# One attention for two sequences, weight sums made on the spot, and a multiply that writes in order: a decoder layer on eight cores

## The chip, the cores and the metric

The kernel runs on all 8 cores of one Trainium2 chip; each core has two sequences of the batch of 16, with no traffic between cores. The time is that of the slowest core, in microseconds (us). An execution is called *slow* when the cores of one die show a lower granted TensorE clock and take over 1% longer than the other die's, or when it is over 1.5% above the fastest of its kernel; all others are *fast*. Only fast executions are compared, except where the text says otherwise.

In lines of the profile PE is TensorE (PEld its weight loads), DVE VectorE, ACT ScalarE, POOL GpSimd, SP the engine that issues most DMA loads and stores; "ps" are PSUM buffers, in which the matmuls leave their results, "M" other buffers. L1555 is line 1555 of the kernel. "A <- B: 32.0, 3, 16.4" says that A waited for B for 32.0 us in all, three times, the longest 16.4 us. The granted clock is the share of full speed at which TensorE was let run.

## The reference, cut to what matters

```python
D_MODEL, BATCH, SEQ, D_FF = 1024, 16, 2048, 2816

def swiglu(x, w_gate, w_up, w_down):
    return (jax.nn.silu(x @ w_gate) * (x @ w_up)) @ w_down

def reference(x, ...):
    h = swiglu(rms_norm(x, ffn1_pre_g), ffn1_w_gate, ffn1_w_up, ffn1_w_down)
    x = x + 0.5 * rms_norm(h, ffn1_post_g)
    # 4 differential heads (dense, causal) and 8 dilated heads; one projection in, one out
    h = hybrid_mixer(rms_norm(x, mix_pre_g), w_in, ..., w_out)
    x = x + rms_norm(h, mix_post_g)
    h = swiglu(rms_norm(x, ffn2_pre_g), ffn2_w_gate, ffn2_w_up, ffn2_w_down)
    return x + 0.5 * rms_norm(h, ffn2_post_g)
```

## The kernel before

Each feed-forward is done in two halves of 1024 tokens. A half is a *gate/up* stage and a *down* stage. Both multiply 2x2 blocks with seven products in place of eight (the Strassen-Winograd scheme), for which sums of weight blocks are needed. Those sums are either made on VectorE from weights just loaded ("raw"), or loaded from main memory, where an earlier stage has stored them. The attention has eight units: 0 to 3 are differential heads, 4 to 7 are pairs of dilated heads. A scheduler in the program places the instructions of each engine in a fixed order ahead of time.

The order of the stages, and the preparation of stored sums, which runs beside the attention:

```python
for s in range(NSEQ):
    half_ffn(s, 0, 0)
    half_ffn(s, 0, 1)
    push_prep(s)            # loads weights, makes sums on VectorE, stores them
    attention(s)
    need(("prep", s))
    half_ffn(s, 1, 0)
    half_ffn(s, 1, 1)
# ...
def push_prep(s):
    if s == 0:
        jobs = [(fi, "d", d, hf) for fi in (1, 0) for d in range(ND) for hf in range(2)]
        jobs += [(0, "g", l, 0) for l in UNSTORED]
    else:
        jobs = [(1, "g", l, 0) for l in UNSTORED]
```

The end of a dilated unit: sums of the exponentials and weighted values lie in PSUM in the order (r, i), with token = 4i + r. The reciprocal is exp(-ln(sum)); the multiply writes the mixed output in token order:

```python
for m in range(2):
    S.op(ACT, lambda e: e.activation(rec[lo], bank(4 + m)[hi], AF.Ln))
S.op(ACT, lambda e: e.activation(rec, rec, AF.Exp, scale=-1.0))
for m in range(2):
    S.op(DVE, lambda e: e.tensor_tensor(
        mixT[lo, u, ts(Q)].rearrange("p (i r) -> p r i", r=4),    # steps of 8 bytes
        bank(4 + m)[lo].rearrange("p (r i) -> p r i", r=4),
        rec[lo].rearrange("p (r i) -> p r i", r=4), ALU.mult))
```

The softmax here doesn't subtract the row's maximum and nothing guards it: scores larger than these inputs give would overflow.

## Time and profile before

| | |
|---|---|
| time, 4 runs | 3062.71 us median (3022.6 to 3089.92) |
| TensorE, VectorE, ScalarE, GpSimd busy | 86, 56, 47, 13% |
| two attentions, with the gap behind each, mean of the eight cores | 603.2 + 564.8 us |
| eight gate/up stages, sum of the cores' medians | 1173.5 us |
| eight down stages, sum of the cores' medians | 614.4 us |

A stage is taken from its first matmul to the first of the next stage, so that the idle time behind it belongs to it. The prediction shows the lines of the profile that these come from. The row of the normalising multiply (line, engine, operation, shapes, count | busy us, mean ns | idle before, and its causes), here of core 5:

```profile
L1555 DVE TENSOR_TENSOR M<-ps,M 64x512 f16<-64x512 f32 x64 | 82.9, 1295 | 108.0 <-ACT M L1551 88.3 <-PE ps L1204 10.8 <-ACT sml L1422 5.2
```

512 elements take 1295 ns, about 2.5 ns each: nearly twice the 688 ns that other operations of this size take (the casts of lines 1213 and 1254).

### The profile page before, as it was taken

How to read it: one execution, taken by the hardware profiler on the slowest of the kernel's cores; microseconds unless marked ns; L12 is line 12 of the kernel's file. 1: busy time of each engine (PE TensorE's matmuls, PEld its weight loads, DVE VectorE, ACT ScalarE, POOL GpSimd, SP SyncE). 2: the span in 40 equal slices, each digit the busy share in tenths (PEclk: the TensorE clock that was granted, in tenths of full speed). 3: DMA queues.
4: the chain of work that ended last, by engine and by line, in shares of the span. 5: the costliest groups of instructions: out<-in, count | busy, mean ns of one | idle time of the engine just before them, and what ended most of it. 6: DMA issues, size and time to landing. Idle time of an engine off the chain costs nothing.

```text
span 3059.0 us, 51439 instructions; the slowest of 8 cores (2993.8 to 3059.0 us)
## 1 busy us (share of the span) xinstructions
PE 2629.8 (86%) x16574; PEld 1345.0 (44%) x16608; DVE 1714.8 (56%) x2918; ACT 1435.0 (47%) x2186; POOL 398.8 (13%) x442
## 2 busy tenths in 40 slices
PE   5999898588986869988999999777898876999996
PEld 2444344355543423333444444654555542344455
DVE  5546634656664675458556465455445556534733
ACT  3434344486643733343354444446764465334432
POOL 1212210112010012102202112001110000110210
PEclk9999999799998977899999999998999998889998
DMA  7766954457477468566477675875212215636868
GB/s 160 153 145 142 187 97 95 108 129 149 90 151 177 108 156 182 162 158 152 122 228 226 199 239 174 269 183 141 75 26 41 44 49 177 188 115 198 268 181 263
DMA packets 241109, 466.94 MB, mean 153 GB/s; under 512 B 39632, under 2 KB 62416, under 8 KB 240848
## 3 DMA queue, kind: packets, MB, share of 16 engines
q1 hardware_dynamic: 203632, 362.90, 38.5%
q0 software_dynamic: 37216, 100.74, 21.1%
q8 instruction: 141, 2.31, 0.3%
q14 instruction: 120, 0.98, 0.1%
HBM read 447.10 MB, written 110.89 MB: 182 GB/s over the span
## 4 chain that ended last, share of the span: by engine, by line
PE 71%; DVE 10%; ACT 7%; issue 7%; DMA 4%; SPq 0%; DVEq 0%; another core or an unknown queue 0%; ACTq 0%; POOL 0%; POOLq 0%
PE ps L989 34%; PE ps L1056 12%; PE ps L1244 6%; PE ps L1092 5%; PE ps L1381 4%; PE ps L1204 3%; PE ps L1342 2%; ACT M L1364 2%; DMA sgu<-M 2%; PE ps L1279 2%; PE ps L1539 2%; ACT M L717 2%; DVE M L1555 2%; DVE M L789 1%; PE ps L1500 1%
## 5 line engine op out<-in xcount | busy, mean ns | idle before, releaser
L989 PE MATMUL ps<-M 128*128 128x512 f16 x4928 | 1150.0, 397 | 119.3 <-DVE M L866 48.9
L989 PEld LDWEIGHTS ps<-M 128*128 128x128 f16 x4928 | 495.5, 101 | 738.3 <-issue 301.2
L1056 PE MATMUL ps<-M 128*128 128x512 f16 (+1 forms) x2464 | 420.7, 333 | 38.5 <-DMA M<-sdn 18.7
L1364 ACT ACTIVATE M<-ps,btab 128x256 bf16<-128x256 f32 (+3 forms) x512 | 349.9, 712 | 141.9 <-PE ps L1342 116.9
L915 POOL TENSOR_TENSOR M<-M 128x512 f16<-128x512 f32 x176 | 234.4, 1332 | 1174.5 <-ACT M L911 1173.5
L719 DVE TENSOR_TENSOR M<-M 128x512 bf16<-128x512 bf16 x336 | 142.7, 425 | 378.4 <-ACT M L717 365.2
L1056 PEld LDWEIGHTS ps<-M 128*128 128x128 f16 x2464 | 244.8, 100 | 204.6 <-issue 56.4
L928 ACT ACTIVATE M<-ps 128x1024 f32<-128x1024 f32 x176 | 180.0, 1023 | 292.3 <-PE ps L989 286.3
L924 DVE TENSOR_TENSOR M<-M,ps 128x512 f16<-128x512 f32 x176 | 120.9, 687 | 317.4 <-PE ps L989 285.2
L1244 PE MATMUL ps<-M 128*128 128x512 f16 x1024 | 260.5, 391 | 32.5 <-DVE M L1444 10.6
L911 ACT ACTIVATE M<-M 128x512 f32<-128x512 f32 x176 | 110.6, 629 | 370.4 <-DVE M L932 370.4
L932 DVE TENSOR_TENSOR M<-ps,M 128x1024 f32<-128x1024 f32 x176 | 214.9, 1223 | 98.0 <-PE ps L989 97.8
L866 DVE TENSOR_TENSOR M<-M 128x1024 f16<-128x1024 f16 (+1 forms) x280 | 217.0, 793 | 61.6 <-DMA sgu<-M 36.3
L717 ACT ACTIVATE M<-M 128x512 bf16<-128x512 f32 (+1 forms) x280 | 165.0, 622 | 146.5 <-DVE M L808 85.8
L1507 ACT ACTIVATE M<-ps 128x1024 bf16<-128x1024 f32 x144 | 140.8, 1006 | 181.0 <-PE ps L1500 159.2
L1204 PE MATMUL ps<-M 128*128 128x128 f16 x2048 | 149.0, 226 | 44.4 <-DVE M L754 38.7
L1381 PE MATMUL ps<-M 128*128 128x129 bf16 x2176 | 177.0, 224 | 9.1 <-DVE M L1368 4.0
L1279 PE MATMUL ps<-M 128*128 128x512 f16 x512 | 126.1, 397 | 55.9 <-ACT M L713 26.0
L789 DVE SCALAR_TENSOR_TENSOR M<-M,gains 128x512 f16<-128x512 f16 x192 | 148.5, 793 | 22.0 <-ACT M L732 21.8
L1381 PEld LDWEIGHTS ps<-M 128*128 128x128 bf16 x2176 | 131.2, 99 | 66.2 <-issue 58.8
L754 DVE SCALAR_TENSOR_TENSOR M<-M,gains 128x512 f16<-128x512 f32 x192 | 132.1, 747 | 44.9 <-ACT M L732 44.6
L1092 PE MATMUL ps<-M 128*128 128x512 f16 x704 | 152.9, 379 | 0.2
(71 smaller groups left out, 2304.1 us busy)
## 6 DMA issues: line engine op xcount, KB each, us to landing
M<-sdn SPq DMA_DIRECT2D x224, 352.0 KB, 4.7
M<-sgu SPq DMA_DIRECT2D x308, 256.0 KB, 3.4
M<-wgu POOLq DMA_DIRECT2D x108, 512.0 KB, 8.0
M<-x SPq DMA_DIRECT2D x96, 512.0 KB, 8.1
sgu<-M SPq DMA_DIRECT2D x66, 512.0 KB, 6.8
M<-xT SPq DMA_DIRECT2D x64, 512.0 KB, 8.9
x<-M SPq DMA_DIRECT2D x64, 512.0 KB, 4.9
sdn<-M SPq DMA_DIRECT2D x48, 352.0 KB, 5.1
```

The lines of the kernel that those rows point to most:

```text
L717: S.op(ACT, lambda e: e.activation(sq[si], src, AF.Square), reads=rd, writes=[B_sq[si]], cost=c_act(512))
L866: eng, lambda e: e.tensor_tensor(SB(j), a, b, op), reads=rd, writes=[bS[j]], cost=cost),
L915: S.op(POOL, lambda e: e.tensor_tensor(hs(p, l), t[:, 0:512], t[:, 512:1024], ALU.mult), reads=bt, writes=[B_H[p][l]], cost=1.3)
L932: S.op(DVE, lambda e: e.tensor_tensor(o, bank(b, 2), o, ALU.add), reads=[B_ps[b], B_ps[b + 1]] + bo, writes=bo, cost=c_dve(1024))
L989: S.op(PE, lambda e, g=g, kc=kc, pb=pb, src=src, piece=piece, n=n: e.matmul(bank(pb + g), src[:, g * 512 + kc * 128:g * 512 + (kc + 1) * 1 ...
L1056: S.op(PE, lambda e, k=k, pb=pb, w=w, piece=piece, n=n: e.matmul(bk(pb), w.ap[:, k * 128:(k + 1) * 128], H[piece][:, k * 512 + c0:k * 512 ...
L1092: S.op(PE, lambda e, k=k, pb=pb, w=w, p=p, c=c: e.matmul(bank(pb), w.ap[:, k * 128:(k + 1) * 128], H[p][:, c * 512:(c + 1) * 512], start=( ...
L1204: S.op(PE, lambda e, kc=kc: e.matmul(bank(pb)[:, tq * 128:(tq + 1) * 128], xn[:, kc, t * 128:(t + 1) * 128], wap[:, kc * 128:(kc + 1) * 12 ...
L1244: S.op(PE, lambda e, kc=kc: e.matmul(bank(pb), wap[:, kc * 128:(kc + 1) * 128], xn[:, kc, ts(tt)], start=(kc == 0), stop=(kc == NKC - 1)), ...
L1279: S.op(PE, lambda e, k=k: e.matmul(bank(pb), wap[:, k * 128:(k + 1) * 128], mixT[:, k, ts(tt)], start=(k == 0), stop=(k == NKC - 1)), read ...
L1364: S.op(ACT, lambda e, o_=o_, i_=i_, bias=bias: e.activation(o_, i_, AF.Exp, bias=bias, scale=SCALE), reads=rd + [B_const], writes=[bP], co ...
L1381: S.op(PE, lambda e, a_ap=a_ap, m=m, uq=uq, first=first: e.matmul(a_ap, P[:, m, uq * 128:(uq + 1) * 128], Vt[i][:, kt, 0:w1], start=(kt == ...
```

## The change

Its intent: keep TensorE fed through the attention. All first feed-forwards come first, then one attention over both sequences, the second's projections filling the first's end, then all second feed-forwards. The preparation leaves the attention: the halves that work on raw weights store their sums. The plain (eight-product) down stages become seven-product ones. Cut to its core (scheduler, buffers and weight ring are left out):

```diff
-for s in range(NSEQ):
-    half_ffn(s, 0, 0); half_ffn(s, 0, 1)
-    push_prep(s); attention(s); need(("prep", s))
-    half_ffn(s, 1, 0); half_ffn(s, 1, 1)
+HALVES = [(s, fi, h) for fi in range(2) for s in range(NSEQ) for h in range(2)]
+RAW  = (tuple(range(NL)), (1, 3, 5, 7, 9), (3, 7), ())     # rows of blocks loaded raw, by half
+KEEP = ((0, 2, 4, 6, 8, 10), (1, 5, 9), (3, 7), ())        # of these, sums stored for later
+for i in range(len(HALVES)):
+    if i == 4: attention()                                  # both sequences
+    half_ffn(i)
+def raw_down(s, h, l):  return (s, h) == (0, 0) or ((s, h) == (0, 1) and l in (0, 2))
+def keep_down(s, h, l): return l in ((1, 3) if h == 0 else (0, 2))

+UORD = (4, 5, 0, 1, 2, 3, 6, 7)             # order of the units; was 0 to 7
+nxt_ = [(s + 1, u, tt) for tt in (lo, hi) for u in UORD[0:2]] if s + 1 < NSEQ else []
+blocks += [..., (s, 6, hi, nxt_[0:1]), (s, 7, hi, nxt_[1:])]

-S.dma_group(SP, prs, ...)                   # 256 copies of 24 KB, dilated values
+S.dma_group(POOL, prs, ...)

-e.activation(ya, bank(pb), AF.Copy)         # mixed output; later a f32 scalar-tensor-tensor
+e.activation(ya, bank(pb), AF.Copy, scale=gains[:, 24 + d:25 + d])   # later a f16 multiply

-    mixT[lo, u, ts(Q)].rearrange("p (i r) -> p r i", r=4),
-    bank(4 + m)[lo].rearrange("p (r i) -> p r i", r=4),
-    rec[lo].rearrange("p (r i) -> p r i", r=4), ALU.mult)
+    mixT[lo, u, ts(Q)].rearrange("p (i r) -> p i r", r=4),
+    bank(4 + m)[lo].rearrange("p (r i) -> p i r", r=4),
+    rec[lo].rearrange("p (r i) -> p i r", r=4), ALU.mult)
```

The four output buffers that the first attention used for its last tiles are taken out too, which leaves two.

## The prediction

> **What bounds the kernel now.** I read the core table first. It sets the yardstick: the time is that of the slowest core, and cores 2 and 3 are some 50 us behind the rest, at a lower granted clock. So I budget on core 5, which ran undisturbed (2993.8 us), and return to the clock at the end.
>
> ```profile
> core 2: 3059.0 us, clock 0.932
> core 3: 3055.1 us, clock 0.931
> core 5: 2993.8 us, clock 0.955
> ```
>
> Then the page's chain of work that ended last: TensorE carries 71% of it, and only in the feed-forward lines (989, 1056, 1092) does it run unbroken.
>
> ```profile
> PE 2629.8 (86%) x16574; PEld 1345.0 (44%) x16608; DVE 1714.8 (56%) x2918; ACT 1435.0 (47%) x2186; POOL 398.8 (13%) x442
> q1 hardware_dynamic: 203632, 362.90, 38.5%
> q0 software_dynamic: 37216, 100.74, 21.1%
> ...
> PE 71%; DVE 10%; ACT 7%; issue 7%; DMA 4%; SPq 0%; DVEq 0%; another core or an unknown queue 0%; ACTq 0%; POOL 0%; POOLq 0%
> ```
>
> The two queue rows (packets, MB, share of 16 engines) say what a byte costs: 0.385 x 3059 x 16 / 362.9 = 52 engine-us per MB on the hardware queue, and 102 on the software queue, whose loads halve f32 to f16. So such a load costs by its source bytes, and 16 engines move 16/52 = 308 MB per ms.
>
> Then core 5 cut at the stage borders (where TensorE's line changes). Columns: stretch, its length, busy time of each engine, clock, DMA share, GB/s.
>
> ```profile
> 32.10:180.50 148.40, 138.14 (x617) 60.16 (x618) 85.44 (x98) 58.66 (x78) 38.98 (x40) 0.99 0.75 161
> 180.50:257.00 76.50, 76.50 (x356) 34.69 (x355) 27.42 (x51) 28.83 (x51) 4.49 (x9) 1.00 0.49 93
> 481.80:1062.50 580.70, 455.77 (x4219) 265.85 (x4218) 349.46 (x702) 332.30 (x512) 65.03 (x94) 0.92 0.55 127
> 1062.50:1083.00 20.50, 1.58 (x19) 0.96 (x16) 11.81 (x22) 6.91 (x12) 0.53 (x1) 0.61 0.71 162
> 1552.40:1687.60 135.20, 133.72 (x620) 60.47 (x619) 82.40 (x117) 62.54 (x85) 29.37 (x22) 1.00 0.72 211
> 1687.60:1755.60 68.00, 66.99 (x311) 30.27 (x310) 34.10 (x63) 31.16 (x54) 0.12 (x1) 1.00 0.68 214
> 1890.70:1986.60 95.90, 73.68 (x621) 61.13 (x620) 48.97 (x97) 42.35 (x89) 3.34 (x7) 0.95 0.95 303
> ...
> 1986.60:2115.00 128.40, 93.18 (x859) 54.05 (x860) 68.79 (x164) 79.16 (x170) 14.27 (x22) 0.91 0.55 125
> 2115.00:2465.00 350.00, 305.01 (x3110) 185.89 (x3108) 190.55 (x373) 207.21 (x259) 24.84 (x35) 0.96 0.22 47
> 2465.00:2529.40 64.40, 50.73 (x250) 22.59 (x251) 39.48 (x70) 37.81 (x71) 0.00 (x0) 0.95 0.29 94
> ```
>
> A gate/up half with stored weight sums takes 135.2 us, 219 ns for each of its 616 matmuls: TensorE-bound. With weights loaded raw and summed on the spot it takes 148.4; a stored down pass 68.0, the plain one 76.5, one split into two column passes 95.9 with the DMA engines at 0.95. The attentions are bound by no engine: TensorE 449 of 543 us and ACT 324 in the second. The middle of it is 87% busy (305.0/350), its entry 73%, its exit 79%. After each come 20 us with TensorE almost empty.
>
> Last, what TensorE waits for from the first attention to the gap behind it:
>
> ```profile
> PE ps L725 <- DVE M L719: 32.0, 3, 16.4
> PE ps L1279 <- ACT M L713: 17.9, 1, 17.9
> PE ps L1539 <- DVE M L1555: 16.4, 17, 1.6
> PE ps L1204 <- DVE M L754: 9.6, 14, 2.5
> ```
>
> The first and last are norm chains at entry and exit; the second is the out-projection held while its buffer serves the weight preparation; the third a slow normalising multiply.
>
> [...]core 2: 0.82 from 2584 to 2773 us[...] cores 0 and 1 of that die had 1.00 and 0.99 then, and long dense stretches elsewhere run at 1.00. [...] 512 f16 elements take 420 ns, 512 f32 ones with a PSUM operand 687. [...]
>
> **The change part by part**, on core 5.
>
> *Order.* Both sequences' first feed-forward now come first, then one attention over both, then the second feed-forwards. The prenorm of the first sequence's attention input runs beside the last down pass; the second sequence's projections fill the first one's end; the second feed-forward's input is ready before attention ends. Today: 580.7 + 20.5 + 542.8 + 19.7 = 1163.7 us. If all attention work ran at the middle's rate: 2 x 448.9/0.871 = 1030. The normalising multiply now writes contiguously: 64 x 1294 ns today, against 687 for a like-sized one with contiguous output; I credit half its two waits of 16 us, 1030 - 16 = 1014. Add 15 us for one cold entry, the handover (the second sequence may not overwrite the mixed output before the first is projected) and the last out-projection: about 1030. Gain 134.
>
> *Preparation leaves attention.* It frees DVE there of about 36 us of 704-element and 34 us of 1024-element sums (64 x 567 ns; 40 x 860 ns); already inside the sum above, as the middle row has none.
>
> *Down passes.* Today: 76.5 + 76.3 (plain), 76.2, 69.2, 68.0, 95.9, 68.1, 78.7 = 608.9 (the third includes a wait at its end). After: eight seven-product passes, two-pass in the last only. The stored ones take 68, but the first half of each feed-forward takes four raw blocks and the second half two of four. Their four opening sums (1408 elements, about 1.1 us each by the 860 ns for 1024) stand on DVE before the second product: +2 to 3 us. Their DMA is heavy: by the program's shapes 11.5 MB of source weights, 5.0 MB stored and 4.2 MB of activations in about 70 us, which is 296 GB/s against the 308 above; I add 3 us more. So 73 + 72 + 68 + 68 and 74 + 72 + 68 + 78.7 = 573.7. Gain 35.
>
> *Gate/up.* Today 148.4 + 148.5 + 163.8 + 160.2 + 135.2 + 135.1 + 145.1 + 135.1 = 1171.4. A raw row of blocks costs (148.4 - 135.2)/11 = 1.2 us. After, the four halves have 11, 5, 2 and 0 raw rows: 149 + 141.5 + 137.5 + 135.2, and with 4 us more behind attention, where norm work remains: 153 + 141.5 + 137.5 + 135.2. Sum 1130.4. Gain 41.
>
> *Moved.* 256 small copies (24 KB) go from SP to GpSimd. At the 544 ns that GpSimd's issue of a projection load takes they are 140 us of an engine that is busy 104 of the two attentions' 1123 us: 9 us per group of 16, mostly while dilated units are projected ahead.
>
> *Sum.* Head and tail unchanged, 32.1 + 17.7 = 49.8; 49.8 + 1030 + 573.7 + 1130.4 = 2784. Other undisturbed cores lie up to 20 us above core 5: 2800. Today's throttled cores pay about 45 us for two returns from attention to dense matmuls (gate/up 184 and 170 instead of 164 and 145 on core 2); after there is one[...]. I add 10. **Predicted 2810 us**, 8% less.
>
> **The rivals.**
> *Attention does not merge well.* A static order, two buffers of Y instead of four, and the rule on overwriting could leave a new 20 to 40 us stall at the handover, or keep the mean at today's 83% (449/543), with 1080 to 1100 us in place of 1030. For it: the waits are many and short (17 on line 1555 in the first attention). Against: the long ones, 15 to 18 us each, are just those the new order removes. Time then 2860 to 2890.
> *DMA becomes the bound in the raw halves.* For it: 296 GB/s estimated against 308. Against: the ring holds two blocks' weights, so a load has about 17 us of lead. If each raw down pass rose to 85 us: +50, 2860.
> [...] each 160 us at 0.81 costs about 30 us. Then 2840 to 2870. [...]
> *GpSimd's copies delay diff units.* The square of line 1414 shares that queue with unit 6's copies; two groups of 9 us per sequence, at most 40 us, if DVE waits behind them.
>
> **Range and chances.** The gains sum to 210 us on one core; 2% needs 61. For less than that two rivals at full size would be needed together. One rival at full size gives 2890; everything going well (1000 for attention, no throttle) gives 2745. So 2745 to 2890, faster 0.95, same 0.04, slower 0.01.
>
> **What would show it.** About 16,200 matmuls (704 plain and 308 of a split pass out, 616 in). One attention stretch of about 1030 us with TensorE 86 to 88% busy and no 20 us gap behind it. No wait of over 10 us on lines 725 or 1279's successors. Down passes 68 to 75 us, only the last split; stored gate/up 135 as now. The normalising multiply near 0.7 us; the mixer's 16-bit scaling 0.42 instead of 0.79. It is wrong if attention stays over 1090, if raw down passes run over 80 with waits on DMA, or if TensorE's own pitch of 219 ns grows.

## The result and the profile after

The changed kernel takes **2920.37 us** (median of 11 runs, 2893.73 to 3176.07); the kernel before, over all its 16 runs of that comparison, 3086.57 (3022.6 to 3274.64). The ratio of the fast runs is 0.9555, 95% interval 0.9507 to 0.9602. A ratio is the mean time of one kernel's fast runs over that of the other's of the same rounds, so it is not quite the ratio of these medians. It is faster by 4.5%, not by the 8% predicted, and outside the predicted range of 2745 to 2890. Four of the eleven runs are slow; the median of the seven fast ones is 2914.56.

The core table of the changed kernel's profiled run (fast), then two lines of its page, the second the chain of waits:

```profile
core 0: 2890.6 us, clock 0.955
core 1: 2910.3 us, clock 0.951
core 5: 2891.5 us, clock 0.959
```

```profile
PE 2571.8 (88%) x16196; PEld 1298.5 (45%) x16196; DVE 1672.7 (57%) x2942; ACT 1441.5 (50%) x2176; POOL 515.1 (18%) x662
...
PE 71%; DVE 10%; ACT 7%; issue 6%; DMA 5%; SPq 0%; POOL 0%; DVEq 0%; ACTq 0%; POOLq 0%
```

The matmuls are the 16,200 predicted. TensorE is busy 88% of the whole span (86% before); the 86 to 88% of the prediction were for the attention alone. The shares of the chain are nearly those of before, so no new engine became the bound. Where the time is missing shows in core 5 cut at its stage borders (same columns as in the prediction):

```profile
184.50:263.70 79.20, 69.56 (x312) 30.29 (x311) 48.05 (x81) 33.00 (x58) 9.30 (x18) 0.98 0.85 195
263.70:406.50 142.80, 137.34 (x619) 61.03 (x620) 96.43 (x135) 60.80 (x82) 36.10 (x33) 0.98 0.85 219
406.50:484.80 78.30, 69.23 (x312) 30.53 (x310) 40.62 (x71) 31.12 (x54) 2.42 (x5) 0.96 0.66 193
484.80:633.20 148.40, 136.67 (x620) 61.06 (x619) 86.54 (x125) 62.65 (x85) 31.26 (x26) 0.95 0.81 225
633.20:701.20 68.00, 66.99 (x312) 30.16 (x311) 33.66 (x63) 30.96 (x54) 0.23 (x1) 1.00 0.62 196
837.50:910.40 72.90, 68.16 (x314) 30.41 (x313) 37.08 (x72) 39.65 (x72) 5.93 (x11) 0.99 0.78 228
910.40:1995.00 1084.60, 905.99 (x8445) 531.95 (x8446) 603.47 (x1296) 671.88 (x1028) 212.52 (x356) 0.93 0.30 74
```

The stored down pass of 68.0 is as predicted. The attention takes 1084.6 instead of 1030, with TensorE busy 906/1084.6 = 84%, not 86 to 88. The third half's gate/up takes 148.4 instead of 137.5, though it has only two raw rows. The raw down passes take 79.2 and 78.3 instead of 73 and 72.

By stages, over the cores (mean for the attention, sum of medians for the others):

| | before | predicted (core 5) | after | after - predicted |
|---|---|---|---|---|
| attention and gap | 1168.0 | 1030 | 1079.1 | +49 |
| gate/up, eight halves | 1173.5 | 1130.4 | 1150.3 | +20 |
| down, eight halves | 614.4 | 573.7 | 597.5 | +24 |

Together +93. Head and tail are 33.3 + 17.6 = 50.9 on core 5 (predicted 49.8), and the sum is 2878. The median of all runs lies 42 above that, where the prediction allowed 26; with these 16 and the 1 of head and tail the missing 110 us are complete. The median of the fast runs alone lies 37 above. In the profiled run the slowest core is core 1, whose seventh gate/up half ran at a granted clock of 0.81 and took 170.9 us against 146 on core 5.

Inside the attention of core 5, three stretches are below the middle's 87% (entry, handover to the second sequence, exit):

```profile
910.00:1010.00 100.00, 76.33 (x711) 49.55 (x711) 67.30 (x107) 39.96 (x53) 37.88 (x70) 0.81 0.50 128
1360.00:1510.00 150.00, 109.96 (x779) 57.21 (x778) 98.47 (x179) 88.48 (x139) 21.50 (x39) 0.85 0.44 127
1860.00:1995.00 135.00, 101.17 (x710) 51.54 (x708) 86.77 (x156) 87.54 (x135) 10.80 (x20) 0.87 0.40 105
```

At a rate of 0.871 the busy time in them would have needed 87.6, 126.2 and 116.2 us. They lose 12.4 + 23.8 + 18.8 = 55 us; the remaining 700 us run 10 better than that rate. In the first two VectorE is fuller than ScalarE; at the exit both are equally full. In all three the granted clock (0.81, 0.85, 0.87) is below the 0.98 of the stretches between them. What TensorE waits for in the whole attention (total us, times, longest):

```profile
PE ps L1597 <- DVE M L1613: 29.2, 29, 3.8
PE ps L1250 <- DVE M L806: 18.7, 16, 6.0
PE ps L776 <- DVE M L770: 16.6, 4, 11.9
```

The first is the normalising multiply, the second the projections that wait for the normalised input, the third the statistics of the norms. The multiply that was to fall to 0.7 us is still the longest wait in total; its row:

```profile
L1613 DVE TENSOR_TENSOR M<-ps,M 64x512 f16<-64x512 f32 x64 | 65.5, 1024 | 92.2 <-ACT M L1609 82.8 <-ACT sml L1473 6.0
```

It takes 1024 ns: the output is contiguous now, but the reciprocal is read in steps of 512 bytes.

### The profile page after: what moved, and what is told of

Its sections match the earlier page's. It is cut to its first block, busy times and chain, and to the rows that moved or that the text cites. A ratio compares the mean times of both kernels' runs of the same rounds, so it can differ in the third digit from the quotient of the medians.

```text
span 2910.3 us, 50541 instructions; the slowest of 8 cores (2869.7 to 2910.3 us)
## 1 busy us (share of the span) xinstructions
PE 2571.8 (88%) x16196; PEld 1298.5 (45%) x16196; DVE 1672.7 (57%) x2942; ACT 1441.5 (50%) x2176; POOL 515.1 (18%) x662
## 4 chain that ended last, share of the span: by engine, by line
PE 71%; DVE 10%; ACT 7%; issue 6%; DMA 5%; SPq 0%; POOL 0%; DVEq 0%; ACTq 0%; POOLq 0%
PE ps L1064 33%; PE ps L1142 15%; PE ps L1291 6%; PE ps L1432 4%; PE ps L1250 3%; PE ps L1328 3%; ACT M L1415 3%; PE ps L1393 2%; PE ps L1597 2%; DVE M L1613 1%; DVE M L925 1%; ACT M L1607 1%; PE ps L1558 1%; DVE M L806 1%; DMA sgu<-M 1%
## 5 line engine op out<-in xcount | busy, mean ns | idle before, releaser
L1064 PE MATMUL ps<-M 128*128 128x512 f16 x4928 | 1114.4, 389 | 70.8 <-DVE M L925 28.6
L1064 PEld LDWEIGHTS ps<-M 128*128 128x128 f16 x4928 | 488.7, 100 | 693.3 <-issue 194.1
L1142 PE MATMUL ps<-M 128*128 128x512 f16 (+1 forms) x2772 | 550.0, 360 | 37.3 <-DVE M L925 21.5
L1142 PEld LDWEIGHTS ps<-M 128*128 128x128 f16 x2772 | 272.3, 99 | 311.4 <-issue 57.4
L1006 ACT ACTIVATE M<-ps 128x1024 f32<-128x1024 f32 x176 | 180.0, 1024 | 270.4 <-PE ps L1064 270.1
L1291 PE MATMUL ps<-M 128*128 128x512 f16 x1024 | 258.3, 388 | 21.5 <-DVE M L1495 6.8
L1565 ACT ACTIVATE M<-ps 128x1024 bf16<-128x1024 f32 (+1 forms) x144 | 141.0, 1009 | 182.2 <-PE ps L1558 160.0
L901 DVE TENSOR_TENSOR M<-M 128x512 f16<-128x512 f16 (+1 forms) x416 | 175.1, 462 | 10.7 <-DVE M L901 0.3
L212 POOL DMA_DIRECT2D M<-M x256 | 141.0, 555 | 226.6 <-DVE M L1264 171.7
L925 DVE TENSOR_TENSOR M<-M 128x1024 f16<-128x1024 f16 (+1 forms) x192 | 166.4, 885 | 15.9 <-DVE M L925 9.3
L1107 ACT ACTIVATE M<-ps 128x512 f32<-128x512 f32 (+3 forms) x144 | 78.9, 549 | 180.8 <-PE ps L1142 169.7
L1301 DVE CAST M<-ps 128x512 bf16<-128x512 f32 x128 | 88.2, 690 | 131.2 <-PE ps L1291 118.2
```

What stands on the lines that cost most here:

```text
L901: S.op(eng, lambda e: e.tensor_tensor(B(o), B(a), B(b), ALU.subtract), reads=bB(a) + bB(b), writes=bB(o), cost=cost)
L925: eng, lambda e: e.tensor_tensor(SB(j), a, b, op), reads=rd, writes=[bS[j]], cost=cost),
L1006: S.op(ACT, lambda e: e.activation(o, bank(b, 2), AF.Copy), reads=[B_ps[b], B_ps[b + 1]], writes=bo, cost=c_act(1024))
L1064: S.op(PE, lambda e, g=g, kc=kc, pb=pb, src=src, piece=piece, n=n: e.matmul(bank(pb + g), src[:, g * 512 + kc * 128:g * 512 + (kc + 1) * 1 ...
L1142: S.op(PE, lambda e, k=k, pb=pb, src=src, piece=piece, n=n: e.matmul(bk(pb), src[:, k * 128:(k + 1) * 128], H[piece][:, k * 512 + c0:k * 5 ...
L1291: S.op(PE, lambda e, kc=kc: e.matmul(bank(pb), wap[:, kc * 128:(kc + 1) * 128], xn[:, kc, ts(tt)], start=(kc == 0), stop=(kc == NKC - 1)), ...
```

## The experiments

There were sixteen runs, in four calls, each on one chip with its own runs of the kernel before. The first call's chip gave a lower clock (0.89 to 0.92 on all cores of its four profiled runs), and nearly all its executions are slow. Its whole times are given but not used; the points were run again. Attention times are means over the eight cores of the profiled run; the changed kernel's is 1079.1.

**1. Third half on stored sums.**

```diff
-RAW  = (tuple(range(NL)), (1, 3, 5, 7, 9), (3, 7), ())
-KEEP = ((0, 2, 4, 6, 8, 10), (1, 5, 9), (3, 7), ())
+RAW  = (tuple(range(NL)), (1, 3, 5, 7, 9), (), ())
+KEEP = ((0, 2, 4, 6, 8, 10), (1, 3, 5, 7, 9), (), ())
```

> The third half of each feed-forward (second sequence, first half) loads only stored weight sums; its two raw rows move their store to the half before. In the changed kernel this half's gate/up takes 146 to 149 us on an undisturbed core, 135 being the stored rate, with one wait of 9 to 10 us on a stored-sum load. Theory A (the mixed layout leaves seven slots for stored sums, so a burst of activation loads at the half's start starves TensorE): the wait goes and each of the two halves falls to 136 to 138 us, the kernel gets 15 to 22 us shorter, with at most 3 us given back in the half before, which stores two rows more. Theory B (the DMA engines are simply full there, at a share of 1.0 for 25 us): the same wait of 8 to 10 us stays, whatever the slots, and the time moves by less than 6 us.

Correct; 3057.79 us, slow. On this chip the third half became equal to the fourth (148.3 and 149.1 us on core 0), where the kernel of run 3, with the raw rows, had 159.5. The wait for a stored block, 9.3 us there on core 0, was gone.

**2. Copies back on SP's queue.**

```diff
-S.dma_group(POOL, prs, B_V[i][tt - 1:tt + 1], [B_VC[i][g]], 400)
+S.dma_group(SP, prs, B_V[i][tt - 1:tt + 1], [B_VC[i][g]], 400)
```

> The 256 small copies go back from GpSimd's queue to SP's. Theory A (on GpSimd a group of 16 takes 9 us to issue and 6 us more to land, and at the handover between the sequences the attention product waits for it): the attention stretch, 1084 us on an undisturbed core, gets 8 to 15 us shorter. Theory B (the copies are issued well ahead nearly everywhere; the profile shows only 3.3 us of matmul waits on them): less than 4 us either way. Theory C ([...] the copies' waits for values hold back weight and activation loads): the stretch gets longer by over 5 us.

Correct; 3074.41 us, all but one execution slow. Attention 1081.6: no effect on it. Run 13 repeats it.

**3. Reciprocal in token order.**

```diff
-e.activation(rec[lo], bank(4 + m)[hi], AF.Ln)
+e.activation(rec[lo].rearrange("p (i r) -> p i r", r=4),
+             bank(4 + m)[hi].rearrange("p (r i) -> p i r", r=4), AF.Ln)
 ...
-    rec[lo].rearrange("p (r i) -> p i r", r=4), ALU.mult)
+    rec[lo].rearrange("p (i r) -> p i r", r=4), ALU.mult)
```

> The reciprocal of the dilated units is written in token order by the logarithm, so the normalising multiply reads it contiguously; PSUM is still read with a stride. In the changed kernel the multiply takes 1.02 us, in the one before 1.29, where I had predicted 0.69. Theory A (the remaining 0.33 us come from the strided read of SBUF): the multiply falls to 0.69 us. Theory B (they come from the strided read of PSUM): it stays at 1.0. If it falls, 32 chains get 0.66 us shorter: attention 5 to 15 us shorter where the chain is exposed (29 us of waits for it now); if the chain's length is set elsewhere, less than 4 us.

Correct; 3081.73 us, slow. Attention 1058.6, 20 us below the changed kernel's, and the multiply at 688 ns. Run 7 has the same edit in fast runs.

**4. Own output buffers at the exit.** The last two output tiles of the second sequence get buffers of their own, as in the kernel before, so that the out-projection needn't wait for the residual adds.

```diff
-yy = [(Y[tt % 2][d], B_Y[tt % 2][d]) for d in range(NKC)]
+far = s == NSEQ - 1 and tt >= 2
+yy = [(YX[tt - 2][d], B_YX[tt - 2][d]) if far else (Y[tt % 2][d], B_Y[tt % 2][d]) for d in range(NKC)]
```

> The last two output tiles of the second sequence are put into two extra buffers again (as the kernel before had), so their projection need not wait for the first two tiles' residual. Theory A (the 25 us in which TensorE is nearly empty at attention's end, from 1940 to 1965 us of the undisturbed core, are that wait: the two output buffers are all in use): the stretch gets 15 to 22 us shorter. Theory B (TensorE waits there in its own order for a statistics matmul whose input VectorE has not summed, and for the norm work of the next feed-forward): the hole stays, only moved behind the last projection, and the gain is under 6 us.

Correct; 3058.71 us, slow. Attention 1061.5 (18 less), but the gate/up half behind it took 171.5 us where run 3, on the same chip, had 155.9. The hole moved. Run 12 repeats it on a better base.

**5. The two attentions one after the other.** The second sequence's projections are added only when the first's output is done, in the otherwise unchanged order.

```diff
-nxt_ = [(s + 1, u, tt) for tt in (lo, hi) for u in UORD[0:2]] if s + 1 < NSEQ else []
+nxt_ = []
+# when the first sequence's blocks are used up: all its outputs first, then the projections
```

> The two sequences' attentions run one after the other again (the first is drained, its output projection included, before the second's first projection); all else as in the changed kernel, whose attention stretch is 1075 to 1085 us on every core so far, undisturbed or throttled. Theory A (my prediction's: most of the stretch's gain came from overlapping the first sequence's end with the second's entry, 30 us or more): the stretch becomes 1110 to 1130 us. Theory B (the handover is hardly overlapped, since it loses 24 us against the rate of the middle as it is): 1085 to 1100 us. Gate/up and down stages as before.

Correct; 3009.82 us median of two fast and two slow runs; fast 2895 and 2897, ratio 0.9529 (0.9451 to 0.9607). Attention 1081.5. Interleaving the sequences gives 2 us: what the diff's main loop was written for is worth next to nothing. Only TensorE's order was made serial; the norm work of the other engines may still run ahead.

**6. Sums of the down weights all made in the first half.**

```diff
-return (s, h) == (0, 0) or ((s, h) == (0, 1) and l in (0, 2))     # raw_down
+return (s, h) == (0, 0)
-return l in ((1, 3) if h == 0 else (0, 2))                        # keep_down
+return True
```

> All four raw blocks' down sums are stored in the first half, so the second half's down pass has no raw blocks. Now on an undisturbed core: first halves 73 to 75 us of pass with 4 us of gap behind, second halves 75 to 78, stored ones 68. Theory A (the loss in a raw pass is its loads and sums: the second half's 7 us wait for a sum is a weight load that lands after 15 us): second halves fall by 7 to 10 us each, first halves rise by 0 to 3 for two more stores, net 10 to 18 us shorter. Theory B (the DMA engines are the bound, as one rival of the prediction had it): the 5 MB of stores that move into the first half lengthen it by 8 us or more, net under 5 us.

Correct; 3007.97 us median of two fast and two slow runs; fast 2901 and 2897. The second halves' down passes fall to 72.5 and 71.4 us (from 76.9 and 76.0), and the third gate/up halves by 3 to 4, but the first halves' grow to 88.8 and 86.9 (from 77.6 and 78.2). TensorE waits there for the weight sums, in the first down pass of core 5 of this experiment:

```profile
PE ps L1142 <- DVE M L925: 13.8, 3, 11.8
```

```profile
DVE M L925 <- DMA M<-wd: 9.1, 1, 9.1
```

In the changed kernel the first line reads 4.3, 3, 2.7, and the second is absent. The sum of 9.1 us waits for raw weights; GpSimd, which issues their loads, had stood 17.4 us before them until a store of sums landed (its trace: DMA sdn<-M). So four blocks' stores in place of two hold up the next loads; the DMA share of that stage is 0.89, and 1.04 or more between 190 and 220 us. Nothing is gained on balance, as the expectation's theory B has it.

**7. Runs 1 and 3 together.** The edits of both.

> The contiguous reciprocal (its run alone: attention 1083 to 1059 us) and the stored third half (its run alone: gate/up of the third half at the stored rate) together. If the two losses are independent, the effects add: attention 1055 to 1062 us and the third halves equal to the fourth ones within 2 us; the kernel some 40 to 47 us below the changed one at the same clock. If the time saved in attention is given back behind it, the gate/up stage after attention grows by 5 us or more over the 152 to 157 us that it takes at this chip's clock.

Correct; **2858.56 us** median of four fast runs and a slow one (fast 2857 to 2859), ratio 0.9402 (0.9354 to 0.945). Attention 1057.4, third gate/up halves 135.9 and 135.9. The multiply's row on core 5, and the wait that had headed the list:

```profile
L1615 DVE TENSOR_TENSOR M<-ps,M 64x512 f16<-64x512 f32 x64 | 44.1, 689 | 89.2 <-ACT M L1611 79.7 <-ACT sml L1473 6.0
```

```profile
PE ps L1597 <- DVE M L1615: 5.4, 14, 0.4
```

29.2 us of waiting became 5.4, but 14.8 us at the same matmuls now go to an exponential (ACT M L1565), which doesn't appear there in the changed kernel: what they wait for in all fell from 48 to 34 us. Writing the reciprocal in the other order costs ScalarE nothing: its logarithm took 591 ns before the edit and 592 after.

**8. The old multiply in the changed kernel.** The three lines of the change's diff that concern it are put back.

> The changed kernel with the old order of the normalising multiply (output strided; 1.29 us each in the kernel before, 1.02 in the changed one, 0.69 with the contiguous reciprocal). If the chain that ends in this multiply sets attention's pace in the dilated units, the stretch answers in proportion: 0.33 us less gave 25 us less, so 0.27 us more should give 18 to 22 us more, about 1100 to 1106 us. If 25 us was an accident of where that one change put the chains, the stretch stays within 8 us of 1084.

Correct; 2922.61 us (fast 2915 to 2924), ratio 0.9607 (0.9545 to 0.9669). Attention 1103.2; the multiply:

```profile
L1613 DVE TENSOR_TENSOR M<-ps,M 64x512 f16<-64x512 f32 x64 | 82.8, 1294 | 93.8 <-ACT M L1609 84.4 <-ACT sml L1473 6.0
```

So three durations give three attention times: 1294 ns, 1103.2 us; 1024 ns, 1079.1; 689 ns, 1057.4. 64 multiplies save 17.3 us of VectorE in the first step and 21.4 in the second; the attention becomes shorter by 24.1 and 21.7. All of it counts. On core 5 one sees how: the waits of the matmuls that weight the values (line 1597) fall from 61 to 48 to 34 us, and TensorE's own busy time, for the same 8,447 matmuls, from 911.0 to 906.1 to 894.5. So besides less waiting the matmuls themselves take less time; the granted clock of the attention is 0.93, 0.93 and 0.94.

Run 8 is also where the prediction's sum can be checked with the old multiply: core 5's attention, then its entry, handover and exit.

```profile
899.40:2001.40 1102.00, 910.96 (x8447) 536.69 (x8448) 620.91 (x1296) 673.09 (x1029) 212.52 (x356) 0.93 0.29 72
...
899.40:999.40 100.00, 73.85 (x684) 47.39 (x685) 67.63 (x103) 38.24 (x51) 37.88 (x70) 0.81 0.46 121
1354.00:1509.00 155.00, 110.85 (x798) 58.74 (x799) 103.43 (x182) 90.88 (x142) 21.51 (x39) 0.87 0.42 123
1866.00:2001.40 135.40, 102.19 (x705) 52.54 (x703) 87.16 (x152) 85.84 (x133) 10.80 (x20) 0.87 0.38 105
```

At the rate of 0.871 the three would need 84.8, 127.3 and 117.3 us. They lose 15 + 28 + 18 = 61 us, and the rest runs 5 better than that rate.

**9. The kernel before with the contiguous multiply alone.** The edits of the change and of run 3 to these lines, and nothing else.

> The kernel before with nothing changed but the normalising multiply of the dilated units: it writes in token order, and the logarithm ahead of it writes the reciprocal in token order too, so that multiply and reciprocal are contiguous (64 multiplies of 1294 ns should become about 690 ns). Theory A, the multiply's time stands on TensorE's path wherever it is, and adds up with the rest of the change: undoing the change's half of it cost 20 us and completing it gained 25 us, so here both together should give 35 to 50 us, ratio 0.984 to 0.989. Theory B, in the old order other waits cover it: under 15 us, ratio above 0.995.

Correct; 3016.28 us (fast 2986 to 3027), ratio 0.9942 (0.978 to 1.0105): by the whole time unclear; in its profiled run cores 2, 3, 6 and 7 had clocks of 0.935 to 0.939 and took 3002 to 3026 us, cores 0 and 1 0.954 to 0.957 and 2957 to 2973. The stages say more: its attentions take 584.6 + 540.8 = 1125.4 us against 1168.0, 42.6 less. Without any new order, this edit gives in the attention nearly what it gives in the new one (1103.2 - 1057.4 = 45.8).

**10. Units in natural order,** on the kernel of run 7.

```diff
-UORD = (4, 5, 0, 1, 2, 3, 6, 7)
+UORD = (0, 1, 2, 3, 4, 5, 6, 7)
```

> The version with stored second-half sums and the reciprocal in token order (2858 us in the batch before), with the units of the attention in their natural order 0 to 7, so the difference units come first as in the kernel before. Theory A, the order of the units matters at the entry and the handover (the change starts with dilated units): attention grows by 10 to 30 us, total 2868 to 2890. Theory B, the losses at entry and handover come from norm chains that every order has: attention within 6 us of 1057, total within 8 us of 2858.

Correct; fast runs 2882 and 2893, two slow, ratio 0.9549 (0.9467 to 0.963). Attention 1079.9, 22.5 more than in run 7. The order of the units matters; that it is not the entry is seen in core 5's first 108 us, where TensorE is busier (92.05/108 = 85%) than in the same stretch of run 7 (85.01/108 = 79%). It loses at the handover: 123.64 us busy of the 180 from 1350, 69%, against 132.22 of 170, 78%, in run 7.

**11. No norm work behind the first sequence's mixer** (wrong result), on the kernel of run 7.

```diff
-po.push(q, xt, DVE, store, tag=("postmix", s, tt))
+po.push(q, xt, DVE, store, tag=("postmix", s, tt), y=s > 0, bare=s == 0)   # bare: no add
```

> Wrong result on purpose: the same version, but the first sequence's mixed output is not scaled and not added to its residual (32 multiplies of 436 ns and 32 adds of about 690 ns taken off VectorE, some 36 us, nearly all of it around the handover from the first to the second sequence; the loads, stores, statistics and matmuls stay). Theory A, VectorE's queue at the handover (0.68 to 0.72 busy there) is what TensorE waits for: attention shrinks by 15 to 30 us, to 1027 to 1042. Theory B, the handover waits for order (mixed outputs that may not be overwritten, loads of the residual, two Y buffers): attention shrinks by less than 6 us.

Wrong (relative error 0.50); 2840.44 us, four fast runs (2839 to 2845), ratio 0.9399 (0.9371 to 0.9426). Attention 1040.4, 17.0 less than in run 7. The handover of core 5 in run 7, then here, 170 us each:

```profile
1340.00:1510.00 170.00, 132.22 (x1026) 71.88 (x1026) 112.38 (x215) 104.40 (x163) 32.05 (x58) 0.89 0.49 143
```

```profile
1330.00:1500.00 170.00, 143.14 (x1171) 78.79 (x1169) 98.98 (x178) 114.20 (x175) 42.60 (x77) 0.94 0.58 169
```

TensorE gains 11 us in this stretch when VectorE loses 13. About half of the 36 us of norm work counts.

**12. Runs 7 and 4 together.**

> The version with stored second-half sums and the reciprocal in token order, and with separate output buffers for the last two output tiles of the second sequence, as in the experiment on the exit: there the buffers took 22 us off attention and gave 15 us back in the first gate/up half behind it. Theory A, the two add up: 2845 to 2853, attention near 1036. Theory B, what the buffers gain is given back behind attention altogether: 2855 to 2862.

Correct; 2855.03 us (fast 2854 and 2855, twice; one slow), ratio 0.9441 (0.9414 to 0.9468). Attention 1036.0, 21.4 less, and the gate/up half behind it 166.0 in place of 147.7, 18.3 more. Core 5's exit hole, TensorE's longest wait in run 7 between 1852 and 1959 us, and what it waits for behind the attention here:

```profile
PE ps L776 <- DVE M L770: 11.9, 1, 11.9
PE ps L1328 <- ACT M L781: 6.2, 1, 6.2
```

```profile
PE ps L1070 <- DVE M L928: 13.6, 10, 3.9
PE ps L1070 <- ACT M L1003: 7.2, 1, 7.2
```

The first of the last two lines isn't all new: in run 7 the same wait was 10.4 us. But VectorE has 120.8 us of work in this half in place of 107.4: the norm work that TensorE no longer waits for at the exit now stands beside the weight sums. The exit's 19 us are real in the attention and worth next to nothing in the whole.

**13. Copies on SP, fast runs,** on the kernel of run 7: the edit of run 2.

> The version with stored second-half sums and the reciprocal in token order (2858 us, attention 1057), with the 256 copies of the dilated values put back from GpSimd's queue to SP's. Theory A, the copies at 555 ns each on GpSimd delay the values of the handover and the entry: attention 8 to 20 us shorter. Theory B, only the issue moves and the dilated units are projected well ahead: attention within 5 us of 1057, total within 8 us of 2858.

Correct; 2865.04 us (fast 2852 to 2888), ratio 0.941 (0.9333 to 0.9487). Attention 1054.4, 3.0 less than in run 7: no effect on the whole.

**14. The mixed output scaled in 32 bit again,** on the kernel of run 7.

```diff
-e.tensor_tensor(yb[d][0], yi[d][0], rst[ri].bitcast(F16)[:, 0:512], ALU.mult)
+e.scalar_tensor_tensor(yb[d][0], yi[d][0], gains[:, gcol + d:gcol + d + 1], rst[ri], ALU.mult, ALU.mult)
```

> The same version with the scaling of the mixed output as in the kernel before: 64 scalar-tensor-tensor operations with a 32-bit factor (about 800 ns) instead of 64 16-bit multiplies (434 ns), 23 us more on VectorE, half of it at the handover and half at the exit. Theory A, VectorE's norm work is on the path there, half of it counts, as when the handover's 36 us were taken off and attention lost 17: attention 9 to 15 us longer. Theory B, it lies beside other work: within 4 us of 1057.

Correct; 2873.1 us (fast 2871 to 2874), ratio 0.9426 (0.9364 to 0.9487). Attention 1064.4, 7.0 more: between the theories. The first down pass of the second feed-forward went from 79.1 to 88.2 as well: on core 5 eight scalings of 750 ns now run into that pass (none in run 7), a weight sum waits 7.8 us for a store of sums (DVE M L920 <- DMA sdn<-M), and TensorE 9.9 us for the sum. The 16-bit scaling is worth 7 us in the attention, and some 15 in the medians of the two calls.

**15. Third half on stored sums, fast runs.** The edit of run 1, beside the changed kernel.

> The changed kernel with the third half's gate/up sums stored already by the second half, and nothing else (a repeat of the first experiment, whose whole times fell in the slow state). Theory A, the loads' lookahead of seven slots is the wait: third halves at 136 instead of 146, second halves 2 us longer, total 15 to 20 us below the changed kernel of the same call, 2893 to 2903. Theory B, it comes back elsewhere: within 6 us of the changed kernel.

Correct; 2898.85 us (fast 2882, 2887 and 2911; one slow), ratio 0.9495 (0.9414 to 0.9576). The third halves fall from 146.3 and 146.5 to 135.9 both, as in run 7. But the second halves' gate/up grows by 1.4 and 2.0, the fourth down pass by 2.9 and the attention by 3.1, and the whole is the changed kernel's. In place of the 15 to 20 us expected, the stages alone give some 10, and the runs don't show it. The wait itself, core 5, third half, in the changed kernel:

```profile
PE ps L1064 <- DMA M<-sgu: 10.3, 1, 10.3
```

In run 7 this line is absent and the stage is 136.0 us.

**16. The changed kernel again,** unedited.

> The changed kernel itself, as the yardstick of this call. Both theories: attention 1079, third halves 146, 2893 to 2921 us in fast runs, ratio 0.950 to 0.960; the improved version's 0.9402 should lie below its interval.

2894.21 us, four fast runs (2892 to 2898), ratio 0.9495 (0.9434 to 0.9557); attention 1079.9.

The version of run 7 beats both kernels: its ratio to the kernel before is 0.9402 against the changed kernel's 0.9555 and 0.9495, and its interval ends below 0.9495. They were run at other times. As 0.9402/0.9495 it would be 1% faster. Run 13 differs from it in the copies alone: 0.941 against 0.9495.

## Why the prediction was right or wrong

**The bound and the direction were right.** TensorE bound, no engine or queue took its place, 16,196 matmuls, stored stages at 68.0 and 135 us as before: each was in the prediction. The gain was sized at 210 us on core 5; the table of stages gives 89 + 23 + 17 = 129 (1168.0 - 1079.1; 1173.5 - 1150.3; 614.4 - 597.5).

**The step that failed first: "Add 15 us for one cold entry, the handover ... and the last out-projection".** With the old multiply the prediction's attention would have been 1030 + 15 = 1045; run 8 measured 1103.2, 58 more. On its core 5 the three places cost 61 us over the middle's rate, not 15: 46 of the 58. Merging was thought to remove what bounds them. Run 5 shows that it doesn't: 1081.5 us serial, 1079.1 merged. At the handover TensorE waits for norm work on VectorE, which has to be done wherever the sequences stand: run 11 took such work away and got 17 us. The exit's wait is worth 21 in the attention, and comes back in the next stage (run 12). The entry was not isolated; its waits in the changed kernel are 10 us for the multiply and 8 for the normalised input.

**A second term of the same sum was short: "2 x 448.9/0.871".** It doubles TensorE's busy time of the second attention, while the first had 455.8 in the prediction's own lines, and run 8 has 911.0. At the rate of 0.871 that is 15 us of the 58; the rest of the attention gives 5 back.

**The multiply's term was mis-sized twice.** "64 x 1294 ns today, against 687 for a like-sized one with contiguous output": the diff makes only the output contiguous, and 1024 ns was measured. "I credit half its two waits of 16 us", 16 us: the waits listed for it understated it. At 1024 ns it gave 24.1 us, and at the assumed duration it would have given 45.8 (runs 7 and 8). The two errors went against each other, which is luck: 1045 + 58 - 16 - 8 = 1079, with the 58 of the first two terms, the 16 credited and 8 more.

The step of the reciprocal costs 1024 - 689 = 335 ns in each multiply, the changed kernel against run 7.

A misreading without weight: the prediction says that its middle row has none of the preparation's sums; it has eight of them, of 1024 elements and 685 ns each.

**Gate/up, +20.** "A raw row of blocks costs ... 1.2 us" held where all or five rows were raw in the first feed-forward (149.9 and 142.6, predicted 149 and 141.5), and failed in the third halves: 146.4 and 145.9 for 137.5, +17. There it isn't the sums that cost but one wait of 10.3 us for a stored block. Within it the granted clock falls to 0.50, with the DMA engines full (core 5 of the changed kernel):

```profile
505.00:510.00 5.00, 2.29 (x6) 0.87 (x7) 3.70 (x6) 0.00 (x0) 0.00 (x0) 0.50 1.06 400
```

The wait is shown by runs 7 and 15; that it's worth little in the whole, by run 15. Their edit takes out the two raw rows and with them the seven fixed slots that a half with some raw rows has for stored blocks, against a ring elsewhere. Which of the two ends the wait was not tested. Full DMA engines alone are not enough for it: in run 7 their share from 490 to 510 us is 0.95 to 1.06 too. The remaining +3 of the table are the sixth stage's +6 and the fifth's -7, and small ones.

**Down passes, +24.** "+2 to 3 us" for the opening sums and "3 us more" for DMA came to 73, 72, 74 and 72; measured 77.6, 76.9, 78.2 and 76.0, so +18. The mechanism was right: run 6 moved the sums and the time went with them, and the waits are those for the sums, there with DMA behind them; the size was off. The fourth down pass takes 73.0 in place of 68 (+5): the norms ahead of the attention now run beside it, which the prediction had taken for free, and on core 5 TensorE waits 3.8 us there for norm work (lines 770 and 781). The remaining 1 or so is the last half's.

**The rivals.** The first named 1080 to 1100 us of attention and a total of 2860 to 2890, and was nearly right in its size (1079, 2920 with the other stages' misses). Of its causes only the handover is shown, and there the norm work more than the rule on overwriting. DMA did not become the bound (no raw down pass of the profiled run over 80 us). GpSimd's copies take 141 us of that engine as predicted, and cost nothing (run 13). The allowance of 26 us over core 5 was short by 16, or by 11 against the fast runs alone.

**What stays open.** The change without its multiply takes 1168.0 - 1103.2 = 65 us off the attention and its gaps. Run 10 puts 22 of that on the order of the units, run 14 some 7 on the scaling, run 5 2 on merging. If these add up, which was not tested, the other 34 were not separated: the preparation taken out, the gap behind each attention, and the order of the norms.

## What to carry to other kernels

Before crediting an overlap, ask what the idle engine waits for in the stretch that is to be filled: if that is another engine's work on the same data, laying two such stretches side by side may fill next to nothing, as here (2 us, run 5), where taking work off that other engine gave 17 us (run 11). For an elementwise operation on the path, check the step of every operand and not of the output alone (the multiply took 1294 ns with a stepped output, 1024 with a contiguous output and a stepped reciprocal, 689 with both contiguous), and let the producer write in the order in which the consumer reads (the logarithm took 591 ns before, 592 after). A wait that is removed from one stage counts only once the whole time shows it; two of these experiments (runs 12 and 15) took 20 us out of stages, and other stages gave back half or more.

## What the runs show of the hardware

- Steps of an operand of VectorE: the multiply of 64x512 elements took 1294 ns with its 16-bit output in steps of 8 bytes and both inputs contiguous (run 8), 1024 with a contiguous output and both inputs in steps of 512 bytes (changed kernel), and 689 when the reciprocal too was contiguous (run 7). In this last form PSUM is still read in steps of 512 bytes, and nothing is seen of it: line 1002, which reads its 512 elements of PSUM contiguously, took 687 in the changed kernel.
- Issuing engine of a DMA: 256 copies moved from GpSimd to SP changed the attention by 3.0 us of 1057.4 (run 13). Each took 555 ns of GpSimd in the changed kernel, 141 us in all, against 1.7 us from issue to landing.
- Granted clock: pairs of cores are seen at 0.81 to 0.83 with the other two of their die at 0.97 or more. Before, from 2584 to 2773 us, cores 2 and 3 had 0.82 and 0.83, cores 0 and 1 1.00 and 0.99. After, from 2440 to 2610 us, cores 0 and 1 had 0.82 and 0.81, cores 2 and 3 0.97; cores 0 and 1 took 167 and 171 us for a stage that took 146 on core 5.
